# Two transformer layers on one core: weight pools, PSUM order and the dealing of w_down changed in five places

## The chip, the cores and the metric

The kernel runs on one core of one Trainium2 chip. The metric is the device time of one execution in microseconds (us). Three runs of the kernel before took 3409.84, 3413.29 and 3413.64 us; the median, 3413.29, is the time that the change is held against. TensorE is called PE here, VectorE DVE, ScalarE ACT, GpSimd POOL, and SyncE, which issues most DMAs, SP.

## The reference

Input x is 2048 rows of 1024 numbers in float32. Two layers follow each other, each with its own weights.

```python
# first block: x -> h = x @ w_in, split into ten parts
y = concat(sgu_mixer(...), conv_module(...), hgrn2_mixer(...))   # each times silu(gate)
x = layernorm(ALPHA * x + y @ w_out) * post_ln_g + post_ln_b
# second block
p = rmsnorm(x, norm1_g) @ w_in_2
mix = concat(pool_mixer(u), diff_attention(dq, dk, dv), stick_breaking_attention(sq, sk, sv))
x = x + mix @ w_out_2
h2 = rmsnorm(x, norm2_g)
x = x + (silu(h2 @ w_gate) * (h2 @ w_up)) @ w_down               # inner width 2816
return rmsnorm(x, final_norm_g)
```

`pool_mixer` takes trailing means of windows of 2, 4, 8 and 16 rows, minus the row itself, and maps each of its four groups of 64 channels with a 64x64 matrix. Both attentions are causal, over 128-query blocks.

## The kernel before, in words

**Numbers.** Matmuls run in float16. Each float32 operand is split into a high and a low half, so that a product takes three matmuls (high by high, high by low, low by high). A row weight comes from DRAM into a float32 staging tile of the pool WS (two tiles; L134), ACT casts its high half (L122), and POOL subtracts to get the low half (L123). The halves lie in the common pool W (five slots of 4 KB a partition) unless the caller names another pool.

**Order of the work.** The program is written in one order, and a tile scheduler reorders it for each engine, by its own simulated time, as far as data and memory allow. A pool that comes to lie on the memory of earlier pools waits for these.

**Stages.** In the order of time: the first block's mixers, to about 783 us; its output projection `out_phase(0)` (from L545), whose matmuls are L588 to L590, to 946; the second block (`block2`, from L706), which runs six attention units one after the other, to about 1983; its output projection `out2` (from L624), to 2122; the feed-forward part's first half `ffn_in`, to about 2990; its second half `ffn_out` (from L1175), to the end.

**`out_phase(0)`.** All eight row weights of w_out are held at once: k = 0 to 4 in W, k = 5 to 7 in a pool `oW0` of three slots. For each of 16 row tiles and each of two column halves, 24 matmuls make one PSUM bank; six banks rotate. DVE adds the residual (L592), takes the statistics, ACT, DVE and POOL normalise twice (layer norm, then the next block's rms norm), and SP transposes the two halves by DMA (L621).

**`block2`.** A unit projects its queries, keys and values (`gemm`; the matmuls are L144 to L146, from PSUM pool `pg`, two banks), stores them, loads keys (L800, L801) and queries, and runs its rows of scores (pool `sc`, four banks) and outputs (pool `apo`, two banks; matmuls L869 and L870 on DMA-transposed probabilities). In units 3 and 4 the generator `pool_mixer` is advanced at two points of each row block (`MIX_ROWS`): a step runs one projection, POOL's running sums, DVE's subtractions (L1018, L1019, L1022), the matmul by the 64x64 maps (L1026) and the store, and ends with `yield`.

**`out2`.** Eight units of two row tiles. For each tile it loads y's two halves (L653) and x (L658), runs 24 matmuls for each of two column halves (L665 to L667; six banks rotate in two pools, two then four), adds x (L668), squares on ACT into a junk bank (L670), stores the sum to x2d (L671), scales the row by its norm (L674) and then forms the sums and differences that a fast matrix product of seven products in place of eight needs (`seven`, `s3`), splits them (L681, L682) and transposes them by DMA (L693), twelve transposes a unit. The norm's weights (`gr`) hold one of the two WS tiles for the whole phase.

**The feed-forward part.** `seven_weights` (from L1056) loads a block of w_gate, w_up or w_down in two staging tiles (L1061, L1062), POOL makes three sums in place (L1068 to L1071), ACT casts (L1074), DVE or POOL subtracts (L1075). The matmuls of `ffn_in` are L1106 to L1108, those of `ffn_out` L1197 to L1199. `ffn_out` goes through w_down in chunks of 3, 3, 3 and 2 sets of weights; within a chunk eight steps `tp` each load one mid tile a set (L1248) and add products to the rows (L1191, L1205, L1207). The next chunk's sets are all asked for at `tp == 1`.

Of the kernel before, what the change touches and what calls it, by code (L numbers as in the profile page):

```python
# [7 lines left out]
F32 = mybir.dt.float32  # L8
F16 = mybir.dt.float16
# [5 lines left out]
PSUM = bass.MemoryType.PSUM  # L15
# [3 lines left out]
D = 1024  # L19
# [19 lines left out]
SCN = 4  # L39
# [27 lines left out]
class Kernel:  # L67
# [477 lines left out]
    def out_phase(self, cw, blk):  # L545
# [3 lines left out]
        wx = self.pool(f"oW{blk}", 3, ctx=cw)  # L549
# [5 lines left out]
        w = [self.row_weight(a[("wo1", "wo2")[blk]], k, None if k < 5 else wx) for k in range(KD)]  # L555
# [68 lines left out]
    def out2(self, cw):  # L624
# [5 lines left out]
        sm = self.pool("usm", 4, ctx=cw)  # L630
        gen = self.pool("gen", 3, ctx=cw)
        yp = self.pool("uy", 8, ctx=cw)
        m = self.pool("um", 5, ctx=cw)
        hp = self.pool("uh", 5, ctx=cw)
        sp = self.pool("us", 1, ctx=cw)
        pq = self.banks("upq", UPQ, cw)
        jp = self.pool("ujk", 1, PSUM, ctx=cw)
# [7 lines left out]
        gr = self.bcast(self.ws, a["n2"], D, "ws")  # L645
        for u in range(4 * NB // 2):
            half, tp = u // 4, u % 4
            xs = []
            for q in range(2):
                y = []  # L650
                for p in range(2):
                    t = yp.tile([128, KD, 128], F16, tag="y", name="y")
                    nc.sync.dma_start(t, self.y2d[2 * half + q][p][:, tp])  # L653
                    y.append(t)
                yh, yl = y
                r = m.tile([128, 2, 512], F32, tag="x2", name="x2")
                rf = r.rearrange("p h n -> p (h n)")
                nc.sync.dma_start(rf, self.x1d[8 * half + 4 * q + tp])  # L658
                ss = sm.tile([128, 2], F32, tag="ss", name="ss")
                for n in range(2):  # L660
                    ns = slice(n * 512, (n + 1) * 512)
                    ps = pq()
                    for k in range(KD):
                        wh, wl = w[k]
                        nc.tensor.matmul(ps, yh[:, k], wh[:, ns], start=k == 0, stop=False)  # L665
                        nc.tensor.matmul(ps, yh[:, k], wl[:, ns], start=False, stop=False)
                        nc.tensor.matmul(ps, yl[:, k], wh[:, ns], start=False, stop=k == KD - 1)  # L667
                    nc.vector.tensor_tensor(r[:, n], r[:, n], ps, ALU.add)  # L668
                    junk = jp.tile([128, 512], F32, tag="junk", name="junk")
                    nc.scalar.activation(junk, r[:, n], AF.Square, accum_out=ss[:, n:n + 1])  # L670
                nc.sync.dma_start(self.x2d[u][:, q], rf)  # L671
                nc.gpsimd.tensor_tensor(ss[:, 0:1], ss[:, 0:1], ss[:, 1:2], ALU.add)
                self.rstd(ss[:, 0:1], ss[:, 0:1], self.eps_rms, 1.0 / D)
                nc.vector.scalar_tensor_tensor(rf, rf, ss[:, 0:1], gr, ALU.mult, ALU.mult)  # L674
                xs.append(r)
# [30 lines left out]
    def block2(self):  # L706
        self.y2d = self.y_scratch("y2d")
        with ExitStack() as c2:
# [5 lines left out]
            self.sm = self.pool("asm", 4, ctx=c2)  # L714
            self.pg = self.pool("pg", PGN, PSUM, ctx=c2)
            self.sc = self.pool("sc", SCN, PSUM, ctx=c2)
            self.po = self.pool("apo", PON, PSUM, ctx=c2)
# [277 lines left out]
    def pool_mixer(self, ct):  # L995
# [6 lines left out]
        for b in range(NB):  # L1002
# [11 lines left out]
            for src, h in ((prev, slice(0, 64)), (cur, slice(64, 128))):  # L1014
                o = P
                if b == 0:
                    first = slice(P, 2 * P)
                    nc.vector.tensor_tensor(cur[h, first], src[h, first], self.invcnt[h, ct, 0:P], ALU.mult)  # L1018
                    nc.vector.tensor_tensor(cur[h, first], cur[h, first], u[h, first], ALU.subtract)  # L1019
                    o = 2 * P  # L1020
                rest = slice(o, P + n)
                nc.vector.scalar_tensor_tensor(  # L1022
                    cur[h, rest], src[h, rest], self.invcnt[h, ct, P:P + 1], u[h, rest], ALU.mult, ALU.subtract
                )
            ps = self.pg.tile([128, 512], F32, tag="pg", name="pm")
# [8 lines left out]
    def ffn(self):  # L1034
# [7 lines left out]
        with ExitStack() as cw:  # L1042
# [3 lines left out]
            self.psums = ((pa, "pa"), (pb, "pb"), (pc, "pc"))  # L1046
            self.wt = self.pool("fwt", 1, ctx=cw)
            self.sp = self.pool("fs", 1, ctx=cw)
            self.mp = self.pool("gm", 1, ctx=cw)
            self.sm = self.pool("gsm", 4, ctx=cw)  # L1050
# [33 lines left out]
    def ffn_in(self, cw):  # L1084
        nc, a = self.nc, self.a
        wx = [self.pool(f"fW{j}", 1, ctx=cw) for j in range(2)]
        sp = self.sp
# [87 lines left out]
    def ffn_out(self, cw):  # L1175
        nc, a = self.nc, self.a
        self.wd = [self.pool(f"wd{j}", 1, ctx=cw) for j in range(max(CHUNKS))]
        sp, sm = self.sp, self.sm
        fg = self.bcast(sp, a["final_g"], D, "s3")
# [41 lines left out]
        def finish(tp):  # L1221
            for q in range(2):
                x = rows[tp][:, q]
                ss = sm.tile([128, 2], F32, tag="fs", name="fs")
                for n in range(2):
                    sq = sp.tile([128, 512], F32, tag="u", name="sq")
                    nc.scalar.activation(sq, x[:, n * 512:(n + 1) * 512], AF.Square, accum_out=ss[:, n:n + 1])
# [10 lines left out]
        for c, n in enumerate(CHUNKS):  # L1238
            nxt = []
            for tp in range(8):  # L1240
                if tp == 1 and c + 1 < len(CHUNKS):
                    nxt = [self.down_weights(at + n + j, c + 1, j) for j in range(CHUNKS[c + 1])]
                pairs = []
                for j in range(n):
                    turn += 1
                    pool, tag = (self.mp, "m") if turn % 6 == 1 else (self.wp, "w")
                    m = pool.tile([128, 14, 128], F16, tag=tag, name="mid")
# [103 lines left out]
```

## Time and profile before

| | |
|---|---|
| median of three runs | 3413.29 us |
| the profiled execution | 3417.88 us |
| its span, first to last instruction | 3416.1 us |
| mean granted clock of PE in it | 0.969 |
| PE busy (matmuls) | 3110.3 us, 91% |
| DVE busy | 2274.2 us, 67% |
| POOL busy | 1357.9 us, 40% |
| ACT busy | 1217.8 us, 36% |

A row of the profile names the line of the kernel, the engine, the operation and its tiles (output, an arrow, inputs). PE's busy time has modelled ends, since its matmuls overlap; the starts are what to go by. "idle before" is the time that the engine had nothing to run before an instruction, with what ended it. A granted clock of 1.00 is 2.4 GHz, 0.50 is 1.2 GHz.

### The profile page before, as it was taken

To read this page: it belongs to the slowest core of one execution; us is meant where nothing else is said; L and a number is where in the kernel's file an instruction comes from. 1 tells how busy PE (TensorE), PEld (TensorE's weight loads), DVE (VectorE), ACT (ScalarE), POOL (GpSimd) and SP (SyncE) were. 2 spreads that over 40 slices of the span, in tenths; PEclk is the share of its full clock that TensorE was granted. 3 is DMA by queue.
4 is the path that set the end of the run, shared out by engine and by line. 5 is a ranking of instruction groups with operands and counts; after the bars stand their busy time and mean duration, and the time that the engine had idled before them with its cause. 6 is when DMAs were issued, how large, how long until landed. Compare 5 with 4: busy or idle time off the path is not lost. (4 is left out here: it accounts for less than half of the span.)

```text
span 3416.1 us, 46957 instructions
## 1 busy us (share of the span) xinstructions
PE 3110.3 (91%) x17736; PEld 1576.9 (46%) x17736; DVE 2274.2 (67%) x3661; ACT 1217.8 (36%) x2291; POOL 1357.9 (40%) x1197
## 2 busy tenths in 40 slices
PE   8999998999988789958779898899999999989998
PEld 4454454785434445534335443344444444434443
DVE  6986979525638888879895744465655656754427
ACT  5223232322124466744564632233222332311103
POOL 5344344403335544565562511332322233244324
PEclk9999999999999899989999999899999999999999
DMA  5102021216756666646645788422222222453324
GB/s 189 38 17 47 13 50 44 58 44 176 179 140 125 125 127 134 134 96 125 127 91 106 154 214 195 117 69 80 80 84 68 74 90 81 161 190 134 110 98 168
DMA packets 597891, 371.85 MB, mean 109 GB/s; under 512 B 500640, under 2 KB 541344, under 8 KB 596640
## 3 DMA queue, kind: packets, MB, share of 16 engines
q1 hardware_dynamic: 590144, 348.22, 40.2%
q10 hardware_dynamic: 7520, 20.63, 1.8%
q8 instruction: 139, 2.28, 0.3%
q14 instruction: 88, 0.72, 0.1%
HBM read 162.70 MB, written 82.31 MB: 72 GB/s over the span
## 5 line engine op out<-in xcount | busy, mean ns | idle before, releaser
L144 PE MATMUL pg<-th,w 128*128 128x512 f16 x1344 | 520.2, 388 | 34.1 <-DVE r L592 11.6
L146 PE MATMUL pg<-th,w 128*128 128x512 f16 x1344 | 518.4, 386 | 7.2 <-POOL w L123 4.0
L145 PE MATMUL pg<-tl,w 128*128 128x512 f16 x1344 | 520.3, 387 | 0.7 <-DVE tl L183 0.7
L869 PE MATMUL po<-v,e 128*128 128x128 f16 (+1 forms) x1088 | 161.4, 252 | 98.6 <-DMA e<-e 85.3
L981 POOL TENSOR_TENSOR e<-e 128x128 f32<-128x128 f32 (+7 forms) x96 | 165.8, 1729 | 196.4 <-DVE e L975 145.8
L845 ACT CAST e<-e 128x1024 f16<-128x1024 f32 (+7 forms) x192 | 150.2, 794 | 224.6 <-POOL e L968 107.0
L846 POOL TENSOR_TENSOR e<-e 128x1024 f16<-128x1024 f32 (+4 forms) x96 | 157.5, 1655 | 180.3 <-ACT e L845 168.2
L145 PEld LDWEIGHTS <-w 128*128 128x128 f16 x1344 | 133.8, 100 | 175.3 <-issue 35.4
L144 PEld LDWEIGHTS <-w 128*128 128x128 f16 x1344 | 133.9, 100 | 171.6 <-issue 16.0
L146 PEld LDWEIGHTS <-w 128*128 128x128 f16 x1344 | 133.7, 100 | 165.8 <-issue 13.5
L975 DVE TENSOR_TENSOR_SCAN e<-e,few 128x129 f32<-128x129 f32 (+7 forms) x96 | 181.5, 1894 | 39.8 <-POOL e L968 31.0
L1075 POOL TENSOR_TENSOR w<-ws,w 128x1024 f16<-128x1024 f32 x20 | 48.6, 2431 | 393.0 <-ACT w L1074 393.0
L1107 PEld LDWEIGHTS <-w 128*128 128x128 f16 x1232 | 121.1, 98 | 172.9 <-issue 32.9
L832 PE MATMUL sc<-k,q 128*128 128x512 f16 (+2 forms) x480 | 174.1, 364 | 28.9 <-DVE e L895 23.7
L1106 PEld LDWEIGHTS <-w 128*128 128x128 f16 x1232 | 121.1, 98 | 165.5 <-ACT w L1074 18.7
L467 DVE SCALAR_TENSOR_TENSOR acc<-h,cols,acc 128x512 f32<-128x512 f32 x240 | 193.4, 826 | 2.4
L900 ACT ACTIVATE e<-e,nm 128x1024 f32<-128x1024 f32 (+4 forms) x192 | 171.1, 892 | 59.7 <-DVE e L895 39.1
L1108 PEld LDWEIGHTS <-w 128*128 128x128 f16 x1232 | 121.1, 98 | 150.0 <-issue 3.5
L833 PE MATMUL sc<-k,q 128*128 128x512 f16 (+2 forms) x480 | 171.7, 365 | 0.0
L869 PEld LDWEIGHTS <-e 128*128 128x128 f16 x1088 | 104.7, 101 | 126.5 <-issue 61.7
L123 POOL TENSOR_TENSOR w<-ws,w 128x1024 f16<-128x1024 f32 x52 | 120.2, 2313 | 96.1 <-ACT w L122 94.2
L870 PE MATMUL po<-v,e 128*128 128x64 f16 (+1 forms) x1088 | 155.3, 211 | 0.0
(318 smaller groups left out, 8018.1 us busy)
## 6 DMA issues: line engine op xcount, KB each, us to landing
mid<-md SPq DMA_DIRECT2D x88, 448.0 KB, 4.1
ws<-in_w SPq DMA_DIRECT2D x48, 512.0 KB, 3.9
md<-mid SPq DMA_DIRECT2D x44, 512.0 KB, 3.4
md<-mid SPq DMA_DIRECT2D x22, 768.0 KB, 5.0
q<-qn SPq DMA_DIRECT2D x96, 128.0 KB, 2.4
ws<-in_wg SPq DMA_DIRECT2D x22, 512.0 KB, 3.5
ws<-in_wu SPq DMA_DIRECT2D x22, 512.0 KB, 4.1
ws<-in_wd SPq DMA_DIRECT2D x22, 512.0 KB, 4.1
```

Of the source, the lines that this page charges most:

```text
L144: nc.tensor.matmul(ps, wh[:, k], th[:, k], start=k == 0, stop=False)
L145: nc.tensor.matmul(ps, wh[:, k], tl[:, k], start=False, stop=False)
L146: nc.tensor.matmul(ps, wl[:, k], th[:, k], start=False, stop=k == KD - 1)
L467: nc.vector.scalar_tensor_tensor(acc[:, ct], src, wcol, acc[:, ct], ALU.mult, ALU.add)
L832: nc.tensor.matmul(ps[:, 0:n], q[:, 0], kk, start=True, stop=False)
L833: nc.tensor.matmul(ps[:, 0:n], q[:, 1], kk, start=False, stop=not last)
L846: eng.tensor_tensor(fv[:, n:2 * n], A[:, 0:n], fv[:, 0:n], ALU.subtract)
L869: nc.tensor.matmul(po, t[:, 0, j], v, start=x == 0, stop=False)
L870: nc.tensor.matmul(po[:, 0], t[:, 1, j], v[:, 0], start=False, stop=x == len(todo) - 1)
L900: nc.scalar.activation(e[r][:, 0:n], e[r][:, 0:n], AF.Exp, bias=nm[:, len(sc) - 1:len(sc)], scale=-1.0, accum_out=ss[:, r, x:x + 1])
L975: nc.vector.tensor_tensor_scan(rev, rev, self.zero.to_broadcast([128, n + 1]), 1.0, ALU.mult, ALU.add)
L981: nc.gpsimd.tensor_tensor(A[:, 0:n], g[:, 1:n + 1], g[:, 0:n], ALU.subtract)
```

## The change

Five things change; the work that is computed stays the same.

1. `out_phase`: weights k = 0 and 1 stay in W, k = 2 to 7 lie in `oW0`, which has six slots.
2. `block2`: the PSUM pools are made in the order outputs, scores, projections, so that `apo` takes banks 0 and 1, `sc` 2 to 5, `pg` 6 and 7 (before: `pg` 0 and 1, `sc` 2 to 5, `apo` 6 and 7).
3. `out2`: the order of its SBUF pools changes, y has six slots in place of eight, the norm's weights have a pool of their own, the junk bank is taken from the other end of PSUM; a unit loads all its tiles first; and the last unit runs k outermost over its four banks.
4. Feed-forward: pools made in another order, `ffn_in` and `ffn_out` with pools of their own for what they shared; mid tiles are padded to 4 KB; the next chunk's w_down sets are asked for one at a time, at odd `tp`.
5. `pool_mixer`: a `yield` stands ahead of its last matmul.

```diff
-        wx = self.pool(f"oW{blk}", 3, ctx=cw)
+        wx = self.pool(f"oW{blk}", 6, ctx=cw)
...
-        w = [self.row_weight(a[("wo1", "wo2")[blk]], k, None if k < 5 else wx) for k in range(KD)]
+        w = [self.row_weight(a[("wo1", "wo2")[blk]], k, None if k < 2 else wx) for k in range(KD)]
...
-        sm = self.pool("usm", 4, ctx=cw)
+        m = self.pool("um", 5, ctx=cw)
         gen = self.pool("gen", 3, ctx=cw)
-        yp = self.pool("uy", 8, ctx=cw)
-        m = self.pool("um", 5, ctx=cw)
+        yp = self.pool("uy", 6, ctx=cw)
+        gp = self.pool("ug", 1, ctx=cw)
         hp = self.pool("uh", 5, ctx=cw)
         sp = self.pool("us", 1, ctx=cw)
+        sm = self.pool("usm", 4, ctx=cw)
         pq = self.banks("upq", UPQ, cw)
-        jp = self.pool("ujk", 1, PSUM, ctx=cw)
+        jp = self.pool("ujk", 1, PSUM, ctx=cw, side="right")
...
-        gr = self.bcast(self.ws, a["n2"], D, "ws")
+        gr = self.bcast(gp, a["n2"], D, "gr")
         for u in range(4 * NB // 2):
             half, tp = u // 4, u % 4
-            xs = []
+            xs, ys, pss = [], [], []
             for q in range(2):
-                y = []
                 for p in range(2):
                     t = yp.tile([128, KD, 128], F16, tag="y", name="y")
                     nc.sync.dma_start(t, self.y2d[2 * half + q][p][:, tp])
-                    y.append(t)
-                yh, yl = y
+                    ys.append(t)
                 r = m.tile([128, 2, 512], F32, tag="x2", name="x2")
+                nc.sync.dma_start(r.rearrange("p h n -> p (h n)"), self.x1d[8 * half + 4 * q + tp])
+                xs.append(r)
+
+            def prods(ps, q, n, k):
+                (wh, wl), (yh, yl), ns = w[k], ys[2 * q:2 * q + 2], slice(n * 512, (n + 1) * 512)
+                nc.tensor.matmul(ps, yh[:, k], wh[:, ns], start=k == 0, stop=False)
+                nc.tensor.matmul(ps, yh[:, k], wl[:, ns], start=False, stop=False)
+                nc.tensor.matmul(ps, yl[:, k], wh[:, ns], start=False, stop=k == KD - 1)
+
+            places = [(q, n) for q in range(2) for n in range(2)]
+            if u == 4 * NB // 2 - 1:
+                pss = [pq() for _ in places]
+                for k in range(KD):
+                    for ps, (q, n) in zip(pss, places):
+                        prods(ps, q, n, k)
+            for q, r in enumerate(xs):
...
+                    if pss:
+                        ps = pss[2 * q + n]
+                    else:
+                        ps = pq()
+                        for k in range(KD):
+                            prods(ps, q, n, k)
                     nc.vector.tensor_tensor(r[:, n], r[:, n], ps, ALU.add)
...
+            self.po = self.pool("apo", PON, PSUM, ctx=c2)
+            self.sc = self.pool("sc", SCN, PSUM, ctx=c2)
             self.pg = self.pool("pg", PGN, PSUM, ctx=c2)
-            self.sc = self.pool("sc", SCN, PSUM, ctx=c2)
-            self.po = self.pool("apo", PON, PSUM, ctx=c2)
...
+            yield
             ps = self.pg.tile([128, 512], F32, tag="pg", name="pm")
             nc.tensor.matmul(ps, self.poolw[:, ct], cur[:, P:P + n], start=True, stop=True)
             self.store(self.y2d, ct, b, ps, self.col("pscale", ct))
...
+            self.mp = self.pool("gm", 1, ctx=cw)
             self.wt = self.pool("fwt", 1, ctx=cw)
-            self.sp = self.pool("fs", 1, ctx=cw)
-            self.mp = self.pool("gm", 1, ctx=cw)
-            self.sm = self.pool("gsm", 4, ctx=cw)
...
-        sp = self.sp
+        sp = self.pool("fs", 1, ctx=cw)
...
+        sp = self.pool("gs", 1, ctx=cw)
         self.wd = [self.pool(f"wd{j}", 1, ctx=cw) for j in range(max(CHUNKS))]
-        sp, sm = self.sp, self.sm
-        fg = self.bcast(sp, a["final_g"], D, "s3")
+        sm = self.pool("gsm", 4, ctx=cw)
+        fg = self.bcast(sp, a["final_g"], D, "fg")
...
             for tp in range(8):
-                if tp == 1 and c + 1 < len(CHUNKS):
-                    nxt = [self.down_weights(at + n + j, c + 1, j) for j in range(CHUNKS[c + 1])]
+                if c + 1 < len(CHUNKS) and len(nxt) < CHUNKS[c + 1] and tp % 2:
+                    nxt.append(self.down_weights(at + n + len(nxt), c + 1, len(nxt)))
...
-                    m = pool.tile([128, 14, 128], F16, tag=tag, name="mid")
+                    m = pool.tile([128, 16, 128], F16, tag=tag, name="mid")[:, 0:14]
```

## Rows read from the trace of the kernel before

**Rows 1.** PE's idle time by what ended it: total us, times, longest us.

```profile
PE po L869 <- DMA e<-e: 85.3, 53, 5.4
...
PE pa L1106 <- ACT junk L670: 17.4, 1, 17.4
...
PE pm L1026 <- DVE win L1019: 14.9, 1, 14.9
...
PE pb L1197 <- DVE x L1191: 12.9, 8, 4.1
...
PE pm L1026 <- DVE win L1022: 10.0, 5, 3.8
```

**Rows 2.** PE's timeline, 946 to 959: start, us, line, [idle before <-releaser].

```profile
958.23 0.59 PE L144 MATMUL pg<-th,w 128*128 128x512 f16 x1 [11.60 <-DVE r L592]
```

**Rows 3.** Timeline around the first output projection: ACT, SP and DVE, by start.

```profile
778.79 1.04 ACT L122 CAST w<-ws 128x1024 f16<-128x1024 f32 x1
...
783.44 0.34 SPq L134 DMA_DIRECT2D ws<-in_wo  x1
...
789.94 1.04 ACT L122 CAST w<-ws 128x1024 f16<-128x1024 f32 x1 [2.41 <-DMA ws<-in_wo]
...
957.50 0.68 DVE L592 SCALAR_TENSOR_TENSOR r<-r,pq 128x512 f32<-128x512 f32 x1
...
983.91 0.56 SPq L800 DMA_DIRECT2D k<-kh  x1
```

**Rows 4.** PE's timeline, 1477 to 1483, at the mixer's first matmul.

```profile
1477.86 2.04 PE L1026 MATMUL pm<-win,poolw 128*128 128x512 f32 x2 [14.92 <-DVE win L1019]
...
1479.70 0.63 PE L144 MATMUL pg<-th,w 128*128 128x512 f16 x1
...
1480.98 0.63 PE L144 MATMUL pg<-th,w 128*128 128x512 f16 x1
...
1482.10 0.38 PE L144 MATMUL pg<-th,w 128*128 128x512 f16 x1
...
1482.75 0.38 PE L144 MATMUL pg<-th,w 128*128 128x512 f16 x1
```

**Rows 5.** Attention's windows: us; PE, PEld, DVE, ACT, POOL busy; PEclk, DMA, GB/s.

```profile
1366.00:1451.40 85.40, 84.67 (x548) 48.14 (x546) 70.52 (x186) 61.12 (x133) 43.13 (x31) 1.00 0.66 134
...
1451.40:1536.80 85.40, 49.70 (x347) 27.19 (x346) 63.02 (x72) 41.87 (x95) 53.48 (x57) 0.84 0.49 97
```

**Rows 6.** The same windows view, for L665 alone, in the attention's tail.

```profile
1890.00:1983.00 93.00, 18.34 (x47) 4.70 (x47) 0.97 0.75 183
...
1966.00:1983.00 17.00, 5.99 (x16) 1.57 (x16) 1.00 0.95 303
```

**Rows 7.** SP's timeline: loads of the second output projection (y: L653, x: L658).

```profile
1891.99 0.71 SPq L653 DMA_DIRECT2D y<-y2d0h  x1
...
1968.84 3.29 SPq L658 DMA_DIRECT2D x<-x1d  x5
```

**Rows 8.** Timeline around the feed-forward's start: DVE, PE, DVE, SP and ACT.

```profile
2138.57 0.68 DVE L668 TENSOR_TENSOR x<-x,pq 128x512 f32<-128x512 f32 x1
...
2140.11 0.58 PE L1106 MATMUL pa<-x,w 128*128 128x512 f16 x1 [17.44 <-ACT junk L670]
...
2146.42 2.53 DVE L674 SCALAR_TENSOR_TENSOR x<-x,ss,ws 128x1024 f32<-128x1024 f32 x2 [7.17 <-DMA x2d<-x]
...
2150.14 0.53 SPq L1062 DMA_DIRECT2D ws<-in_wg  x1
...
2161.39 1.47 ACT L1074 CAST w<-wt 128x1536 f16<-128x1536 f32 x1 [3.66 <-POOL wt L1071]
```

**Rows 9.** Timeline in ffn_out: SP and PE.

```profile
3034.30 0.33 SPq L1061 DMA_DIRECT2D ws<-in_wd  x1
...
3035.91 14.10 SPq L1248 DMA_DIRECT2D mid<-md  x6
...
3042.65 0.61 PE L1197 MATMUL pa<-wd,mid 128*128 128x512 f16 x1 [4.22 <-DMA mid<-md]
```

More of the change, by code (lines that the diff above doesn't have):

```diff
@@ L653, in out2 @@
                     nc.sync.dma_start(t, self.y2d[2 * half + q][p][:, tp])
-                    y.append(t)
-                yh, yl = y
+                    ys.append(t)
                 r = m.tile([128, 2, 512], F32, tag="x2", name="x2")
+                nc.sync.dma_start(r.rearrange("p h n -> p (h n)"), self.x1d[8 * half + 4 * q + tp])
[12 more added lines that the diff above has]
+            for q, r in enumerate(xs):
                 rf = r.rearrange("p h n -> p (h n)")
-                nc.sync.dma_start(rf, self.x1d[8 * half + 4 * q + tp])
                 ss = sm.tile([128, 2], F32, tag="ss", name="ss")
                 for n in range(2):
[L661 to L667, printed above, removed]
+                    if pss:
[4 more added lines that the diff above has]
+                            prods(ps, q, n, k)
                     nc.vector.tensor_tensor(r[:, n], r[:, n], ps, ALU.add)
@@ L674, in out2 @@
                 nc.vector.scalar_tensor_tensor(rf, rf, ss[:, 0:1], gr, ALU.mult, ALU.mult)
-                xs.append(r)
             s3 = sp.tile([128, 3, 512], F32, tag="s3", name="s3")
@@ L1225, in finish @@
                 for n in range(2):
-                    sq = sp.tile([128, 512], F32, tag="u", name="sq")
+                    sq = sp.tile([128, 512], F32, tag="sq", name="sq")
                     nc.scalar.activation(sq, x[:, n * 512:(n + 1) * 512], AF.Square, accum_out=ss[:, n:n + 1])
```

## The prediction, made before the changed kernel was run

> **What bounds the kernel now.** I read first which waits ended TensorE's (PE's) idle time, then the timelines around the longest ones, then windows of equal length. In the sum of waits, one long repeated wait stands out, the attention's L869 on its transposing DMAs, 85.3 us in 53 pieces; nothing in the diff touches it. Four others lie where the diff works: 17.4 us once at the start of the feed-forward part, 14.9 us once and 10.0 us in five pieces at the pooling mixer's matmul L1026, and 12.9 us in eight pieces in `ffn_out` [rows 1]; the gap at the head of the second block's projections, 11.60 us, has a row of its own [rows 2]. A wait that ends in one instant tells only what was late last, so each is followed one step back below. The profiled execution took 3417.88 us with a span of 3416.1 and lies 4.6 us above the median of the runs, 3413.29; the sum is made against it and then set on the median.
>
> A unit used throughout: at full speed the wide matmuls start 0.65/3 = 0.217 us apart, in the half-speed stretch 1.28/3 = 0.427 [rows 4].
>
> **Part 1, weights of the first output projection.** Weights k=2 to 4 leave the common pool W for the phase's own pool, which overlaps the memory of the phase before; so six casts wait for that phase instead of three. Before, the first such cast ran at 778.79, one staging tile had then to be refilled at 783.44, and the last weight was cast at 789.94: 6.5 us from refill to cast [rows 3]. After, six weights wait and two staging tiles hold two of them, so four refills follow, two at a time: the last cast comes between one more round (+6.5 us) and, SP and POOL taking them one by one, some 10 us later. Every psum of the phase needs all eight weights, so that delay is on the path of the phase, PE's 48 matmuls a tile (10.4 us) being its pace. At the other end the block gives something back. PE waited 11.60 us until the last add of the phase, L592 at 957.50, had emptied the psum bank that the next projection's pool takes [rows 2, 3]; the change lets that pool lie in two banks that the phase doesn't use, and W's three freed slots let its weights come earlier. But PE can't run away with this: the attention's keys are loaded by L800 only at 983.91 [rows 3], behind the phase's last transposes on SP, and these move with the delay. Bounds: the gap wholly gained and half the delay hidden, -11.6 + 6.5 = -5; the whole delay and nothing gained, +10. I take **+4**, nearer to the delay because the load of the keys is on the delayed chain and the gap isn't.
>
> **Part 2, the mixer.** A `yield` puts L1026 and its store one step later; the extra instructions are none, and the eight steps that were used in the first half of a unit are now used over all of it. At 1477.86 PE had waited 14.92 us for L1019, and the matmuls queued behind it, L144 first, had nothing to do with the mixer; the clock was then at its lower level for two microseconds more (half-speed spacing until 1482.10, six matmuls, 1.3 us lost) [rows 4]. Not all of it is the kernel's loss, since attention is paced by the vector engines too. The window with the stall has VectorE busy 63.02 of 85.4 us against 70.52 in the one before, and PE 49.70 against 84.67 [rows 5]. Counted by VectorE's lost work, (70.52-63.02)/0.826 = 9.1 us is what the kernel lost, where 0.826 is 70.52/85.4. The five other pieces add 10.0 at most [rows 1]. Bounds: -26 (all of 14.9 + 10.0 + 1.3) and 0, if the scheduler, which orders by its own clock, puts the matmul back in front. I take **-10**: the 9.1 and a tenth of the rest.
>
> **Part 3, second output projection and the feed-forward's start.** This loses something first. Before, the projection's matmuls filled PE's holes in the attention's tail: L665 has 47 records by 1983, 16 of them after 1966 [rows 6], and three matmuls go with each, so 141 matmuls or 30.6 us; the y tiles came from 1891.99, while the x tiles, in memory that the attention's pool U held, came at 1968.84 [rows 7]. After, y tiles overlap U too and can't come before about 1969, and the first two psums lie on the attention's output banks, which are the last to be freed. So 31 x 3 x 0.217 = 20.2 us of fill is lost, 30.6 if the scheduler doesn't let the other psums go ahead. Against that stands the 17.44 us hole at 2140.11 [rows 8], which this lost fill simply pushes into: PE would end the phase 20 us later, at about 2143, and be kept less long. What then ends last? Before, the last add L668 ran at 2138.57, the rows' last scaling L674 at 2146.42 after 7.17 us for the x2d store, the second tile of w_gate was issued at 2150.14 because its staging slot was held by the norm's weights, and the sum weights' cast came at 2161.39: 22.8 us from the add [rows 8]. The change gives the norm's weights a pool of their own, so w_gate comes early; the sum weights still lie over this phase's x tiles, so they wait for the last of these. I count 20 us for the same tail: last add at 2143.5, cast at 2163.5, **+2** against 2161.39. The junk bank's move lets 36 matmuls that need no sums (7.8 us) start at once, though PE did such ones before, too. The last unit with k outermost closes its four psums together: four adds of 0.68 and the squares and stores in one row, +0 to +8; that it frees the weights' slots in W one by one ends no wait above. Taken: **+3**. Bounds: -14 (the 17.44 hole goes and only 3 us are given back) and +21 (the rival below).
>
> **Part 4, w_down dealt over a chunk.** In place of three sets at the chunk's second step comes one set at each odd step. The same loads and casts run, so nothing is added in work; one set blocks SP for less. Before, the loads of a set were issued at 3034.30 after their slot came free, the mid tiles behind them on SP at 3035.91, and PE waited 4.22 us for one at 3042.65 [rows 9]. That wait should go. Of the 12.9 us on L1191 [rows 1] a part is queued behind the sets' work on POOL. Bounds: -17 (4.2 + 12.9) and +2, sets now being late for their chunk. I take **-6**: 4.2 and an eighth of 12.9. The larger mid tiles change no instruction.
>
> **Sum.** +4 - 10 + 3 - 6 = -9: 3417.88 - 9 = 3408.9 for the profiled execution, and 3413.29 - 9 = **3404** for the median. Own range of this case, with the halves of the bounds: 3392 to 3416.
>
> **A rule that would speak against the change.** In the attention, scores and outputs change psum bank every few matmuls, and in the window from 1366 PE is busy 84.67 of 85.4 us at a granted clock of 1.00 [rows 5]. The Trainium skill, TensorE: Matmul & The Clock Gate, section "A second HAM failure mode: psum-queue depth-cycling", says that a kernel whose matmuls go round the psum banks in each iteration had its clock fall and rise between bursts. By that rule the last unit, four banks in turn every three matmuls, would run at the lower clock; the trace's row disagrees.
>
> **Rivals.**
> - *Slower: the lost fill is charged (0.22).* Place: from the attention's last transposes to the first feed-forward matmul. It decides once the lost fill exceeds the 17.44 us hole. At 30.6 us [rows 6] PE ends 13 us beyond the hole, and the k-outermost unit adds up to 8: +21 in place of +3, so 3404 + 18 = 3422. For it: y tiles over U, the first two psums on the last banks freed. Against it: four other psums can run ahead.
> - *The holes really close (0.15).* The projection gains 11.60 in place of +4, and the feed-forward's start 17.4 in place of +3: -9 - 15.6 - 20.4 = -45, 3368. Against it: the load of keys at 983.91 and the sum weights behind the x tiles.
> - *The change doesn't do what it says (0.13).* The scheduler keeps L1026 and the sets where they were: parts 2 and 4 are nil, +7, 3420. For it: it reorders everything, as the 47 early L665 show.
> - *The clock falls in the last unit (0.03).* 96 matmuls at 0.427 in place of 0.217 cost 20.2 us: 3424. The row on the attention speaks against it.
>
> **The numbers.** The forecast has 0.47. A measurement of this kernel tells about 0.2%, 6.8 us, from no change. Of the forecast's 0.47 some 0.29 lies below 3406.5, 0.17 within the bound and 0.01 above; with the second rival faster has 0.45. Same takes the 0.17, half of the third rival and a fifth of the first, 0.27, and slower the rest, 0.28. The range takes in the slow rivals and leaves out most of the second: 3380 to 3428.
>
> **What would show it.** Right: L1026 with no wait over 3 us and the 1451 window's PE near 60 us; a projection's first matmul within 2 us of the phase's end, but keys no earlier than 984; L665 only after 1969 and PE's end of the phase near 2143; no wait on mid near 3042. Wrong: the first feed-forward matmul straight after the phase's last and the sums' cast before 2155 (then the second rival), or after 2170 (the first); the mixer's stall in another place.

## The result: slower by 1.35%, and the profile after

The changed kernel took 3458.26 us (median of four runs, 3453.79 to 3462.94) beside 3412.1 of the kernel before: a ratio of 1.0135, interval 1.012 to 1.015, so 46 us slower. The forecast was 3404, its range ended at 3428. The profiled execution, the fastest of the four, spans 3452.0 us beside 3416.1; its 36 us are what the rows can account for. One run of e10 below (4608.56 us, at a mean granted clock of 0.652 where its others have 0.96) is left out of that run's median.

Where they came in is read from the first and last starts of four groups of matmuls, in the view of instructions by line (median duration, first to last start). Of before and of after, in pairs:

```profile
L869 PE MATMUL po<-v,e x1088: 216/272/421, 1012.1 to 1972.6; 128*128 128x128 f16 x91, 128*128 128x256 f16 x91
...
L665 PE MATMUL pq<-w,y x256: 377/379/631, 1897.5 to 2121.9; 128*128 128x512 f16 x128
...
L1106 PE MATMUL pa<-x,w x176: 376/379/631, 2140.1 to 2932.4; 128*128 128x512 f16 x176
...
L1197 PE MATMUL pb<-wd,mid x264: 376/379/634, 2948.3 to 3405.1; 128*128 128x512 f16 x132
```

```profile
L881 PE MATMUL po<-v,e x1088: 216/272/422, 1029.2 to 1989.9; 128*128 128x128 f16 x91, 128*128 128x256 f16 x91
...
L661 PE MATMUL pq<-w,y x256: 378/379/632, 1991.1 to 2166.9; 128*128 128x512 f16 x128
...
L1117 PE MATMUL pc<-x,w x176: 378/379/635, 2175.2 to 2985.6; 128*128 128x512 f16 x176
...
L1209 PE MATMUL pb<-wd,mid x264: 376/379/635, 2988.5 to 3441.0; 128*128 128x512 f16 x132
```

The lag is 17.1 us at the attention's first output matmul, still 17.3 at its last, 45.0 at the end of the second output projection, 35.1 at the first feed-forward matmul, 40.2 at the first of `ffn_out` and 35.9 at its last. So the first output projection lost 17, and the attention (and with it the mixer) lost and gained nothing. The second output projection lost 28, the shorter wait ahead of the feed-forward part gave 10 of them back, and 5 more went in `ffn_in`: 23 in all. `ffn_out` gained 4.

PE's waits by what ended them, after (total us, times, longest), for [rows 1]:

```profile
PE po L881 <- DMA e<-e: 69.6, 35, 6.2
...
PE pg L144 <- DVE kl L809: 27.5, 3, 20.7
PE pm L1039 <- DVE win L1031: 14.1, 2, 13.8
PE pq L588 <- DVE r L592: 11.0, 4, 6.4
PE pb L1209 <- DVE x L1203: 10.2, 10, 3.0
...
PE pm L1039 <- DVE win L1034: 8.2, 4, 3.0
...
PE pa L1209 <- DMA mid<-md: 4.6, 1, 4.6
```

The 11.6 us before the projections are gone, and 20.7 us at the same boundary have come, behind another instruction; the waits on L588 are new, and the mixer's are as they were.

Around the first output projection, after (timelines of ACT, DVE, PE and SP), for [rows 2, 3]:

```profile
774.66 1.98 ACT L122 CAST w<-ws 128x1024 f16<-128x1024 f32 x2
...
795.90 1.05 ACT L122 CAST w<-ws 128x1024 f16<-128x1024 f32 x1 [1.08 <-DMA ws<-in_wo]
...
805.47 1.29 DVE L592 SCALAR_TENSOR_TENSOR r<-r,pq 128x512 f32<-128x512 f32 x2 [12.74 <-PE pq L590]
807.28 1.27 DVE L592 SCALAR_TENSOR_TENSOR r<-r,pq 128x512 f32<-128x512 f32 x2
...
856.91 0.58 PE L588 MATMUL pq<-w,y 128*128 128x512 f16 x1 [6.42 <-DVE r L592]
...
978.28 0.67 DVE L592 SCALAR_TENSOR_TENSOR r<-r,pq 128x512 f32<-128x512 f32 x1
...
989.89 0.58 PE L144 MATMUL pg<-th,w 128*128 128x512 f16 x1 [20.68 <-DVE kl L809]
...
999.14 0.58 SPq L812 DMA_DIRECT2D k<-kh  x1
```

The last weight is cast 6 us later than before. The adds of the first two row tiles come almost together, at 805.47 and 807.28, and the phase's last add is at 978.28 where the instructions by line have 958.8 for before. Before, the second tile's first add lay just as close behind the first tile's (797.10), but its second add came 5 us later:

```profile
798.89 0.67 DVE L592 SCALAR_TENSOR_TENSOR r<-r,pq 128x512 f32<-128x512 f32 x1
...
803.89 0.68 DVE L592 SCALAR_TENSOR_TENSOR r<-r,pq 128x512 f32<-128x512 f32 x1
```

PE's first kind of matmul in this phase by line, before and after:

```profile
L588 PE MATMUL pq<-w,y x256: 379/379/379, 779.8 to 945.8; 128*128 128x512 f16 x128
```

```profile
L588 PE MATMUL pq<-w,y x256: 376/379/632, 775.7 to 958.0; 128*128 128x512 f16 x128
```

Before, PE went through the phase in 166.0 us and waited for nothing; after, it took 182.3.

The mixer's first matmul and the window around it (us; PE, PEld, DVE, ACT, POOL busy; PEclk, DMA share, GB/s), after, for [rows 4, 5]:

```profile
1493.85 2.04 PE L1039 MATMUL pm<-win,poolw 128*128 128x512 f32 x2 [13.78 <-DVE win L1031]
```

```profile
1467.40:1552.80 85.40, 51.24 (x340) 28.96 (x339) 65.15 (x70) 40.67 (x92) 55.81 (x56) 0.76 0.48 94
```

The second output projection: its first kind of matmul alone in the attention's tail, as a window, then SP's loads of x and y, for [rows 6, 7]:

```profile
1890.00:2000.00 110.00, 4.55 (x12) 1.17 (x12) 0.80 0.66 158
```

```profile
1907.92 2.98 SPq L656 DMA_DIRECT2D x<-x1d  x5
...
1985.53 0.58 SPq L653 DMA_DIRECT2D y<-y2d0h  x1
```

None lies ahead of the attention's last output matmul now; the 12 are those from 1991.1 on. Before, it was 31 records, 93 matmuls, of the 47 that [rows 6] has by 1983: the last output matmul starts at 1972.6, and the 16 records after 1966 all come behind it. Before, L665 alone:

```profile
1890.00:1946.00 56.00, 5.91 (x16) 1.56 (x16) 0.99 0.70 171
...
1946.00:1966.00 20.00, 6.43 (x15) 1.58 (x15) 0.91 0.71 115
...
1966.00:1972.60 6.60, 0.00 (x0) 0.00 (x0) 1.00 0.99 225
```

x, which used to wait for the attention's memory, comes 61 us earlier, and y, which used to come at 1891.99, waits for it in x's place.

The feed-forward's start and `ffn_out`, after (DVE, PE, ACT, SP, PE), for [rows 8, 9]:

```profile
2173.27 2.47 DVE L681 TENSOR_TENSOR x<-x,pq 128x512 f32<-128x512 f32 x4
...
2175.20 0.59 PE L1117 MATMUL pc<-x,w 128*128 128x512 f16 x1 [7.53 <-DVE x L681]
...
2182.92 2.55 DVE L687 SCALAR_TENSOR_TENSOR x<-x,ss,gr 128x1024 f32<-128x1024 f32 x2 [7.18 <-DMA x2d<-x]
...
2195.43 1.47 ACT L1085 CAST w<-wt 128x1536 f16<-128x1536 f32 x1 [4.31 <-POOL wt L1082]
...
2196.96 0.61 PE L1117 MATMUL pb<-x,w 128*128 128x512 f16 x1 [6.95 <-ACT w L1085]
...
3075.52 12.05 SPq L1260 DMA_DIRECT2D mid<-md  x6
...
3081.71 0.61 PE L1209 MATMUL pa<-wd,mid 128*128 128x512 f16 x1 [4.61 <-DMA mid<-md]
```

The 17.44 us hole is one of 7.53 now, the four adds of the k-outermost unit come together at 2173.27, the sum weights are cast at 2195.43 (2161.39 before), and the wait on the mid tile, which dealing the sets was to end, is still there.

### The profile page after: what moved, and what is told of

Its sections match the earlier page's. It is cut to its first block, busy times and chain, and to the rows that moved or that the text cites. A ratio compares the mean times of both kernels' runs of the same rounds, so it can differ in the third digit from the quotient of the medians.

```text
span 3452.0 us, 46929 instructions
## 1 busy us (share of the span) xinstructions
PE 3129.8 (91%) x17736; PEld 1584.1 (46%) x17736; DVE 2269.2 (66%) x3661; ACT 1219.9 (35%) x2291; POOL 1367.0 (40%) x1197
## 5 line engine op out<-in xcount | busy, mean ns | idle before, releaser
L844 PE MATMUL sc<-k,q 128*128 128x512 f16 (+2 forms) x480 | 178.6, 374 | 42.3 <-DVE e L907 32.4
L987 DVE TENSOR_TENSOR_SCAN e<-e,few 128x129 f32<-128x129 f32 (+7 forms) x96 | 182.3, 1903 | 38.8 <-POOL e L980 30.3
L845 PE MATMUL sc<-k,q 128*128 128x512 f16 (+2 forms) x480 | 177.1, 376 | 0.0
L123 POOL TENSOR_TENSOR w<-ws,w 128x1024 f16<-128x1024 f32 x52 | 119.4, 2298 | 105.8 <-ACT w L122 100.0
```

The source lines that it names most:

```text
L844: nc.tensor.matmul(ps[:, 0:n], q[:, 0], kk, start=True, stop=False)
L845: nc.tensor.matmul(ps[:, 0:n], q[:, 1], kk, start=False, stop=not last)
L987: nc.vector.tensor_tensor_scan(rev, rev, self.zero.to_broadcast([128, n + 1]), 1.0, ALU.mult, ALU.add)
```

## The experiments

All are held against the kernel before on the same chip (its median was 3412.8 to 3415.3 in the five sets of runs); a ratio has its 95% interval.

### One part at a time

**e1: the weights alone.**

```diff
-        wx = self.pool(f"oW{blk}", 3, ctx=cw)
+        wx = self.pool(f"oW{blk}", 6, ctx=cw)
...
-        w = [self.row_weight(a[("wo1", "wo2")[blk]], k, None if k < 5 else wx) for k in range(KD)]
+        w = [self.row_weight(a[("wo1", "wo2")[blk]], k, None if k < 2 else wx) for k in range(KD)]
```

> The kernel before with part 1 of the change alone (w_out weights k=2 to 7 in oW0, six slots). In the changed kernel's trace the attention's first output matmul comes 17.2 us later than before (1029.24 against 1012.05). Theory A (the weights that wait for the first block's end make the row chain start later and fall into a slower pace): the whole of that comes from this part, so about +17, 3429 us, and L592's last instruction near 978 instead of 958.8. Theory B (the order of the PSUM pools moves this boundary, since the projection's banks differ): this part alone gives 0 to +5, 3412 to 3417. My forecast's own term was +4.

Measured: 3429.04 us, ratio 1.0045 (1.0029 to 1.0062), +16. L592's last start is 978.6. Theory A.

**e2: the new `out2` alone** (the diff of `out2`, with the rest as before).

```diff
...
+        m = self.pool("um", 5, ctx=cw)
         gen = self.pool("gen", 3, ctx=cw)
-        yp = self.pool("uy", 8, ctx=cw)
-        m = self.pool("um", 5, ctx=cw)
+        yp = self.pool("uy", 6, ctx=cw)
+        gp = self.pool("ug", 1, ctx=cw)
...
```

> The kernel before with the new out2 alone (pool order, six y slots over U, norm weights in a pool of their own, loads first, last unit k outermost); PSUM order of block2 and the feed-forward pools as before. Theory A (the y tiles over U can't be loaded until the attention's last tiles are freed, so all 141 filling matmuls are lost): y loads only after about 1965, +20 to +28, 3432 to 3440 us. Theory B (the fill is lost because the first two psums lie on the attention's output banks): with the old PSUM order the fill stays, some 40 or more L665-type matmuls before the attention's end, and the time is within 8 us of before, or faster by the 10 us that the changed kernel gains at the feed-forward's start.

Measured: 3435.1 us, 1.0062 (1.0047 to 1.0077), +22. The first y load:

```profile
1965.53 0.58 SPq L653 DMA_DIRECT2D y<-y2d0h  x1
```

The first L661 is at 1971.0, behind the attention's last output matmul at 1970.6: with the old PSUM order, too, the whole fill is gone. Theory A; B falls as the cause of this loss.

**e3: yield and dealing alone.**

> The kernel before with the mixer's yield and the dealing of the w_down sets alone (and the padded mid tiles). Theory A: the yield moves nothing, the mixer's first matmul still waits about 14 us; dealing gives 4 to 6 us in ffn_out; 3406 to 3409 us. Theory B: the yield does move the stall and the gain was hidden in the changed kernel by its other parts: 3396 to 3402 us.

Measured: 3412.89 us, 0.9997 (0.9987 to 1.0006): nothing. The mixer's first matmul (L1027 there) waits for L1019 as before:

```profile
PE pm L1027 <- DVE win L1019: 14.9, 1, 14.9
```

The wait on the mid tile is 3.4 us, from 4.2. Theory A for the mixer; the 4 to 6 us of the dealing didn't show in the time.

**e4: the changed kernel without the weights' part.**

> The changed kernel with part 1 undone (weights k=0 to 4 in W, three slots in oW0), everything else as changed. Theory A: 17 us come back, 3441 us, the attention's first output matmul within 3 us of 1012. Theory B (PSUM order): it stays near 1029 and the time near 3458.

Measured: 3429.27 us, 1.0049 (1.0033 to 1.0064). Theory A, and more than its 17: 29 us come back by the medians, 23.7 by the spans of the two profiled executions (3452.0 and 3428.3). 20.7 of the 23.7 lie ahead of the attention's last output matmul (1989.9 and 1969.2), where e1 alone lost 14.3 (1986.9 beside 1972.6); the runs that leave the weights and the mixer's wait as they were have that matmul between 1969.2 and 1976.0. e1 and e2 alone make 38 of the 46. Why the weights cost more in the changed kernel than alone isn't shown.

### What the weights did

**e5: six slots, but three weights in them.**

```diff
-        wx = self.pool(f"oW{blk}", 3, ctx=cw)
+        wx = self.pool(f"oW{blk}", 6, ctx=cw)
```

> The kernel before with oW0 given six slots but still only k=5 to 7 in it, so that only the addresses of the phase's later pools move. Theory A (the loss of 16 us in e1 comes from the weights that wait and must be refilled): nothing is lost, 3412 plus or minus 6 us, L592's last start near 959. Theory B (the row tiles, pushed to higher addresses, lie on memory that the first block frees later, or the schedule of the row chain changes with them): about +10 to +16, 3423 to 3429 us.

Measured: 3413.78 us, 0.9997 (0.9987 to 1.0006). The addresses do nothing; the weights do.

**e12: four weights in four slots** (k < 4 in W).

> The kernel before with four weights of the first output projection in its own pool (k=4 to 7) in place of three; six of them cost 16 us (e1). Theory A (each further refill makes the row chain start later, and the loss goes with the delay): one more weight means one refill more, the last cast 2 to 3 us later, +2 to +6, 3415 to 3419 us. Theory B (a threshold: the row chain falls out of its staggered order at any delay): +10 to +16, 3423 to 3429. Theory C (hidden up to a point): within 2 us of before.

Measured: 3407.13 us, 0.9976 (0.9966 to 0.9986), 8 us *faster*, which no theory had. The phase before ends earlier: the first L588 is at 773.9 beside 779.8. In the profiled executions of the six kernels that free a slot of W (the changed one, e1, e12, e15, e16, e17) it is at 773.5 to 776.0, in the others at 778.3 to 782.4, so the freed slot fits as the reason. The first add comes at 792.63 and the last at 951.6, 18.7 and 177.7 us behind that first matmul, where before has 17.3 and 179.0.

**e16: e1 with a third row tile.**

```diff
-        m = self.pool(f"om{blk}", 2, ctx=cw)
+        m = self.pool(f"om{blk}", 3, ctx=cw)
```

> e1 (six weights in the phase's own pool, 3429 us) with three row tiles in flight in place of two (om0 three slots). Theory A (the late start sets two row tiles off together, and with two slots the next two can only be loaded when both are through; the chain goes in pairs at 11.5 us a tile in place of 10.4): the third slot takes the loss away, 3404 to 3414 us, and L592's last start is near 955 or earlier. Theory B (the loss is the later start itself, or the next block's weight casts that now run on ACT and POOL beside the chain): 3422 to 3430 us.

Measured: 3402.15 us, 0.9968 (0.9955 to 0.998): the loss of 16 is a gain of 13 by the medians, 11 by the ratio. Theory A. The adds of the first output projection, by line, in before, e1 and e16, one fence each:

```profile
L592 DVE SCALAR_TENSOR_TENSOR r<-r,pq x32: 668/679/689, 797.1 to 958.8; 128x512 f32<-128x512 f32 x32
```

```profile
L592 DVE SCALAR_TENSOR_TENSOR r<-r,pq x32: 669/682/690, 803.3 to 978.6; 128x512 f32<-128x512 f32 x32
```

```profile
L592 DVE SCALAR_TENSOR_TENSOR r<-r,pq x32: 662/680/690, 803.1 to 950.6; 128x512 f32<-128x512 f32 x32
```

e1 and e16 start alike, 6 us late. From the first add to the last go 175.3 us in e1 and 147.5 in e16 (161.7 before). So what cost was the chain's pace with two row tiles after the late start, 175.3/15 = 11.7 us a tile, slower than PE's 10.4; that a third tile mends it is shown. Before with a third row tile was not run, so e16 doesn't tell what the late start costs when three tiles are in flight. Why the pace fell is not shown. The first two tiles' adds start 1.8 us apart in e1 (803.29 and 805.10), but so they do before (797.10 and 798.89) and in e12 (792.63 and 794.44), which keep their pace. The first add, though, comes 29.8 us behind the first L588 in e1, 17.3 before and 18.7 in e12.

### What shut the fill out

**e6 and e7: the new `out2` with y ahead of x again** (the edit is against e2's order); e7 has the last unit in the plain order as well.

```diff
-        m = self.pool("um", 5, ctx=cw)
         gen = self.pool("gen", 3, ctx=cw)
         yp = self.pool("uy", 6, ctx=cw)
+        m = self.pool("um", 5, ctx=cw)
         gp = self.pool("ug", 1, ctx=cw)
```

> The kernel before with the new out2 (norm weights in a pool of their own, loads first, last unit k outermost, junk bank on the other side) but its pools in the order gen, uy (six slots), um, ug, so that y lies where it lay before and x lies over U. Theory A (y's place alone costs the fill): y loads come from about 1892 again, some 47 L665-type records lie before 1983, PE's wait at the feed-forward's start shrinks from 17.4 to about 8 us, and the time is 3400 to 3410 us. Theory B (something else of the new out2, the loads ahead of the matmuls or the k-outermost unit, costs the 22 us of e2): 3425 to 3435 us.

> As e6, with the last unit in the plain order (k innermost, one psum after the other). Theory A: the k-outermost unit costs 4 to 8 us at the feed-forward's start, since its four adds come together, so this is faster than e6 by that. Theory B: the k-outermost unit frees the w_out weights' slots early and the feed-forward's weights follow, so this is slower than e6 by a few us.

Measured: e6 3412.37 us, 0.9989 (0.998 to 0.9999); e7 3410.87, 0.999 (0.9981 to 1.0). The 22 us are back, so y's place was e2's whole loss; k outermost, with y in this place, costs or gives nothing that can be told. The 8 us more that I had expected from the feed-forward's start didn't come: there PE's wait is at most 3.8 us, but PE now waits for y inside `out2` (in e6 6.53 us at 2030.61, 4.93 at 2103.61).

**e10, e10b: the changed kernel without the weights' part and with y ahead of x; in e10b the PSUM order is put back too.**

```diff
-            self.po = self.pool("apo", PON, PSUM, ctx=c2)
-            self.sc = self.pool("sc", SCN, PSUM, ctx=c2)
             self.pg = self.pool("pg", PGN, PSUM, ctx=c2)
+            self.sc = self.pool("sc", SCN, PSUM, ctx=c2)
+            self.po = self.pool("apo", PON, PSUM, ctx=c2)
```

> The changed kernel with part 1 undone and y put back ahead of x in out2's pools; its PSUM order, the dealing, the yield and the feed-forward pools stay. Theory A (weights and y's place are the whole loss): 3405 to 3413 us. Theory B (the PSUM order, by which the first two psums of out2 lie on the attention's output banks, keeps a loss of its own): 3418 to 3428 us, with clearly fewer than 47 of the first out2 matmuls of each triple before the attention's end.

> As e10, with block2's PSUM order also put back. Theory A: as e10, within 4 us. Theory B: 10 us or so faster than e10, 3405 to 3413 us.

Measured: e10 3433.7 us, 1.0059 (1.0045 to 1.0073); e10b 3414.1, 1.0005 (0.9996 to 1.0014). The first matmuls of `out2` (L661 alone) between 1880 and 1970, in e10 and in e10b (us, PE busy and count, PEld busy and count, PEclk, DMA share, GB/s):

```profile
1880.00:1970.00 90.00, 6.11 (x17) 1.66 (x17) 0.81 0.68 147
```

```profile
1880.00:1970.00 90.00, 13.41 (x32) 3.44 (x33) 0.94 0.68 150
```

In e10, y is there early (L653 at 1890.50), but the first L661 runs at 1948.7, when DVE has read a bank of scores. Fifteen records are missing beside e10b, 45 matmuls or 9.8 us: half of the fill is lost, not all. And PE waits for a y tile inside `out2`, where e10b's longest such wait is 9.1 us:

```profile
2048.36 0.61 PE L663 MATMUL pq<-w,y 128*128 128x512 f16 x1 [17.02 <-DMA y<-y2d0l]
```

So the PSUM order by itself costs about 20 us as well (19.6 by the medians, 18.3 by the spans), once y is in place. Theory B in both, with more than the 10 us that I had put on it.

**e15: the changed kernel with the PSUM order alone put back.**

> The changed kernel with block2's PSUM order alone put back. Theory A (y over U shuts the fill out by itself, so the PSUM order matters only once y is back): 3452 to 3464 us, as the changed kernel. Theory B (the two add up): 21 us less, near 3437 us.

Measured: 3449.37 us, 1.0099 (1.0085 to 1.0113). By medians 9 to 12 us come back, by the spans (3452.0 and 3448.3) 3.7; the first L661 is still after the attention's last output. Nearer theory A, as the time from the attention's last output matmul to the end of the span shows (us, one profiled execution each):

| run | y lies over U | PSUM order changed | last output matmul | span | between them |
|---|---|---|---|---|---|
| before | no | no | 1972.6 | 3416.1 | 1443.5 |
| e6 | no | no | 1969.8 | 3411.2 | 1441.4 |
| e10b | no | no | 1973.7 | 3415.2 | 1441.5 |
| e10 | no | yes | 1971.7 | 3433.5 | 1461.8 |
| e2 | yes | no | 1970.6 | 3433.3 | 1462.7 |
| e15 | yes | no | 1987.5 | 3448.3 | 1460.8 |
| e4 | yes | yes | 1969.2 | 3428.3 | 1459.1 |
| after | yes | yes | 1989.9 | 3452.0 | 1462.1 |

Two locks on one door: either costs about 20 us, both together no more, and opening one alone gives next to nothing.

### What the mixer's wait is worth

**e8: L1026 reads the copied projection u; the window work runs, and its result is left out of the output.**

```diff
-            nc.tensor.matmul(ps, self.poolw[:, ct], cur[:, P:P + n], start=True, stop=True)
+            nc.tensor.matmul(ps, self.poolw[:, ct], u[:, P:P + n], start=True, stop=True)
```

> The kernel before, with the mixer's matmul L1026 reading the copied projection u in place of the window differences: the window work still runs, but its result is left out of the output, and PE no longer waits for it. It prices the mixer's stall. Theory A (my term: the kernel loses 9 to 10 us by the waits on L1026): 3400 to 3404 us. Theory B (attention is paced by the vector engines there, the stall is hidden): within 4 us of before. Theory C (PE's loss counts in full): 3388 to 3392 us.

Measured: 3396.59 us, 0.9952 (0.9936 to 0.9968), -16 by the ratio and -18 by the medians, of the 24.9 us that PE waits there. Between A and C: the term was real and larger than I had put it.

**e9: yield, and an order edge behind the row's last output matmul.**

```diff
-            nc.tensor.matmul(po[:, 0], t[:, 1, j], v[:, 0], start=False, stop=x == len(todo) - 1)
+            self.spread_end = nc.tensor.matmul(po[:, 0], t[:, 1, j], v[:, 0], start=False, stop=x == len(todo) - 1)
...
+            yield
...
-            nc.tensor.matmul(ps, self.poolw[:, ct], cur[:, P:P + n], start=True, stop=True)
+            with self.tc.issue_after(self.spread_end.ins):
+                nc.tensor.matmul(ps, self.poolw[:, ct], cur[:, P:P + n], start=True, stop=True)
```

> The kernel before with the mixer's yield and, beside it, an order edge that queues L1026 on PE behind the last output matmul of the row that was written ahead of it. Theory A (the yield was right in its aim, but the scheduler puts the matmul back, because by its own clock the window is ready sooner than on the chip): the wait of 14.9 us at the first L1026 falls below 3 us and the time comes near that of the run in which the matmul reads u, 3397 to 3403 us. Theory B (the mixer's wait only moves to another instruction, since the attention's vector work is the bound there): 3409 to 3414 us.

Measured: 3467.15 us, 1.0159 (1.0146 to 1.0173): the waits on L1026 are gone from the list, and 54 us are lost. The wait sits on the output matmuls instead (L869 on its DMAs: 105.8 us, longest 13.9, where [rows 1] have 85.3 and 5.4), and the attention ends 50 us later. **e11**, the same edge on e10b, did the same:

> As e10b, with the order edge for L1026 of e9. If the terms add up: the time of e10b less what e9 gains, 3392 to 3402 us, faster than the kernel before and the changed one.

Measured: 3462.35 us, 1.0148 (1.0133 to 1.0164). Both expectations fell. The edge also pins what is queued behind L1026; which of that costs the 54 us wasn't followed further.

**e13: the mixer's next projection written ahead of L1026, no yield.**

```diff
-            nc.scalar.copy(u[:, P:P + n], self.gemm_ct(w, b))
+            nc.scalar.copy(u[:, P:P + n], ahead if b else self.gemm_ct(w, 0))
...
+            if b + 1 < NB:
+                ahead = self.gemm_ct(w, b + 1)
             ps = self.pg.tile([128, 512], F32, tag="pg", name="pm")
```

> The kernel before, with the mixer's next projection (24 matmuls of L144 to L146) written ahead of L1026, without the change's yield; the same instructions in another order. Theory A (what costs is that matmuls which don't depend on the window are queued behind L1026): part of the 16 us that the unwaiting matmul of e8 gave comes back, 3400 to 3408 us. Theory B (any other order only moves the wait, as the edge of e9 did): 3411 us or more.

Measured: 3388.3 us, 0.9922 (0.9909 to 0.9936), -27: theory A, by more than its range. PE's waits in e13 (total, times, longest):

```profile
PE po L869 <- DMA e<-e: 72.7, 37, 6.6
...
PE pm L1028 <- DVE win L1022: 6.2, 4, 4.1
...
PE pm L1028 <- DVE yl L206: 1.8, 1, 1.8
...
PE pm L1028 <- POOL hn L189: 1.2, 1, 1.2
```

The 14.9 us wait on L1019 is gone, and the attention's last output matmul is at 1947.6 beside 1972.6. The gain is larger than in e8, but not in the attention: there that matmul is at 1949.0, nearly as early. The difference of the two runs lies behind the attention, 1438.1 us to the end of the span here and 1446.6 in e8 (1443.5 before), and isn't attributed further.

**e14: e7 with e13's mixer. e17: e14 with four weights, as e12.**

> e7 (repaired out2, which stood about 2 us below before) with e13's mixer. If the terms add up, 2 to 4 us below e13; faster than the kernel before and than the changed one if e13 is.

> e14 (3384 us) with four weights in the phase's own pool, as e12, which was 8 us faster than the kernel before. If the terms add up: 3376 to 3379 us. If e12's gain came from a row chain that is no longer late for something here: 3382 to 3386 us.

Measured: e14 3384.13 us, 0.9909 (0.9896 to 0.9923); e17 3383.25, 0.9913 (0.9899 to 0.9926). Both are faster than the kernel before by 31 to 32 us and than the changed one by 74 to 75. e14 is 4 us below e13, as expected if the terms add up; e12's gain does not add to e14's, the second of e17's two cases.

## Why the prediction was wrong

**Part 1 (+4; measured 17).** Four refills came, as forecast, and the last cast ran at 795.90 beside 789.94, near the lower of my two ends. From the phase's first such cast to its last it was the upper end: 21.2 us (from 774.66) in place of 11.2 (from 778.79), 10 us more, of which 4 were made up since the phase before ended earlier. The step that failed is the one that took PE's 48 matmuls a tile as the pace of the phase, so that a delay at its start would come out at its end no larger. PE did keep that pace before, 166.0 us for sixteen tiles without a wait. But the phase ends with its adds, and these are paced by the chain of the row tiles, (958.8 - 797.1)/15 = 10.8 us a tile against PE's 10.4, which six banks hid from PE. After the late start they went at 11.5 us a tile ((978.3 - 805.5)/15), so that 8.4 us at the first add became 19.5 at the last; DVE's waits on the loads of row tiles ahead of them rose from 12.8 to 23.1 us, and PE, its banks full, waited 11.0 us for them. e16 shows that a third row tile takes this loss away; why two fall behind after this start stays open. That the 11.60 us gap wouldn't be gained was right (the add at 957.50 that ended it is the last but one; the last is at 958.82): the load of the keys moved from 983.91 to 999.14, and PE waited 20.68 us at a later matmul of the projections.

**Part 2 (-10; measured 0).** The term's size was too small rather than too large (16 us in e8, 27 in e13's order). What failed is that the edit would do what it says: for the mixer the third rival, given 0.13, was the case. In e3, where it stands almost alone, the same instruction waits the same 14.9 us. A yield only changes the order in which the program is written. e13 changes only that order too, and there the wait went; why the scheduler kept the matmul's place in the one and not in the other isn't shown.

**Part 3 (+3; measured 23).** The lost fill was put at 20.2 us, 30.6 at most. It was 20.2, 31 records of three matmuls 0.217 us apart; the 30.6 counts 16 records behind the attention's last output matmul, which were no fill. PE's end of the phase moved further, by 27.7 us (45.0 - 17.3): PE waited 6.9 us inside `out2`, mostly for y tiles, where it was 2.6 before, and the rest isn't attributed. The step that failed is that this lost fill "simply pushes into" the 17.44 us hole, with the last add at 2143.5, right behind PE's end. In the trace PE's last matmul starts at 2167.3, the last add at 2175.1 and the sums' cast at 2195.4. Less the 17.3 us carried in, that is 2150.0, 2157.8 and 2178.1, where the prediction had 2143, 2143.5 and 2163.5. The tail from the add to the cast was right, 20.3 us for 20. Before, the adds of `out2` never waited for PE; after, they waited 16.0 us, so the chain behind them moved with the late matmuls, and the four adds of the last unit come after all of these. The hole gave back 9.9 us (17.44 to 7.53). Beyond that `ffn_in` lost 5 (35.1 to 40.2); PE's waits on its weights' casts rose from 2.7 to 8.8 us (6.95 at 2196.96). The first rival had place and direction right, and its sign came: the cast lies behind 2170 even without the 17.3 us. It was given 0.22. Its sum isn't what ran, since it took the fill as 30.6, the hole as wholly closed and up to 8 for the k-outermost unit, of which e6 beside e7 shows nothing; that its +21 lies near 23 is luck. The rival of the falling clock didn't come: in the last unit (2145 to 2167.5) the granted clock was 1.00.

**Part 4 (-6; measured -4).** The size was near by luck, since the reason wasn't: the wait on the mid tile stayed (4.61), and the waits on the adds, 12.9 us before, came to 10.2. Alone (e3) no gain can be told, and where the 4 us came from stays open.

**The sum.** 17 + 0 + 23 - 4 = 36, the span's difference; the medians differ by 46, and single runs of the changed kernel lie up to 9 us apart, of the kernel before up to 12 in one set. The range failed since it held the slow rival only as an alternative to a forecast with +4 and -10 in it. Parts 1, 2 and 3 all came out at or beyond their bad bounds, which I had treated as separate cases. (The chances stated for faster and same, 0.45 and 0.27, add up to 0.44 and 0.28 from their parts.)

## What to carry to other kernels

When work of the next stage fills a stage's idle slots, look at every resource that lets it in, SBUF address and PSUM bank alike. Here either one on memory that is freed last cost about 20 us, y's place by shutting out all of the fill, the PSUM order by half of it and a longer wait on y; mending one alone showed next to nothing. A phase whose row chain is as slow as its matmuls (10.8 us a tile beside 10.4) can lose its slack by a later start though PE never waited before; here a further row tile in flight took that loss away. And writing a waiting matmul later in the program didn't move it, while writing ready work ahead of it ended the wait: read the new order from the trace rather than from the program.

## What the runs showed that I had not expected

One wait of PE has a price that its own length doesn't tell: 24.9 us of waiting at the mixer were worth 16 us when it was taken away (e8), 27 us when ready matmuls were put ahead (e13), and -54 us when it was moved behind a row (e9). At the attention's last output matmul the first two gain nearly the same, 23.6 and 25.0 us; they part behind it. And with one slot of the common pool freed (e12) the phase *before* ended 6 us earlier (first L588 at 773.9 beside 779.8), a gain at a place that my working had not looked at.
